# Taking the two-operand elementwise work of one kernel off GpSimd, and opening a stage's PSUM pools in another order

## The chip, the cores and the metric

The kernel runs on one core of a Trainium2 chip. The metric is device time in microseconds, measured from outside the program; the median of three runs is what a version is judged by. One more execution was profiled, and every row below is from that one. [...]

## The reference

One sequence of 512 tokens of width 1024 goes through two blocks in float32. Cut to the order of the work:

```python
# block 1
h = _rms_norm(x, norm_mix_pre);  z = h @ w_in_first
attn = _rms_norm(_dilated_attention(q, k, v), attn_out_gain)
rw = _rwkv7(...)                                  # recurrent scan, 8 heads of 64
mixed = concatenate([attn, rw]) @ w_out
x = x + _rms_norm(mixed, norm_mix_post)
h = _rms_norm(x, norm_ffn_pre)
f = square(relu(h @ w_ffn_up)) @ w_ffn_down       # 1024 -> 4096 -> 1024
x = x + _rms_norm(f, norm_ffn_post)
# block 2
proj = rmsnorm(x) @ w_in                          # conv, q, k, v, gates
x = x + (sigmoid(gate_c) * conv_out + sigmoid(gate_a) * attn_out) @ w_out
x = x + cross_attention(rmsnorm(x), rmsnorm(mem), ...)
x = x + hierarchical_moe(rmsnorm(x), ...)         # 16 experts, two of them per token
return rmsnorm(x, norm_final_g)
```

## The kernel before, in words

**Products.** Activations lie transposed in SBUF (`hT`, 128 features by 512 tokens per tile, two halves of 256 tokens where a norm comes first). A float32 matrix product is made of three products of split operands: hi by hi, lo by hi, hi by lo (lines 371 to 373 with the tokens as the streamed side, lines 380 to 382 with the weights on it). So each weight chunk of 128 x 1024 that a DMA brings (`wl`) is split by `wsplit`: ScalarE (ACT) copies it to a rounded `hi` (L354), and `lo = t - hi` is one elementwise subtraction with two operands in SBUF (L357):

```python
nc.scalar.activation(hi, t, AF.Copy)
self.nsplit += 1
eng = nc.gpsimd if self.nsplit % 4 in SP[self.stage] else nc.vector
eng.tensor_tensor(lo, t, f32(hi), ALU.subtract)
```

The table `SP` (L53) says, by stage, which of four consecutive subtractions go to GpSimd (POOL) and which to VectorE (DVE): two in four while the first mixer's projections, the FFN, the second mixer and the cross-attention's output weights are loaded; all four for the first mixer's `w_out` (whose product runs among the steps of the recurrent scan, `rw_run`) and for the cross-attention's query weights; none for the first low-rank chunk and for the experts. Activations are split in the same manner after a transpose: ACT writes the hi part (L426), DVE the lo part (L427).

**Norms.** A norm that stands behind a product (`post_norm`, L1023 to L1035) handles four row tiles `t` of 128 tokens, twice in block 1 (after `w_out`, on `mix`, and after the FFN, on `f`). For `t` in `PN` (0 and 1), POOL multiplies the tile with the gain (L1029, `mg`), and DVE then does one instruction (L1032). For the other two, DVE does two (L1034: tile times 1/rms times gain; L1035: added to `x`). 1/rms itself is a run of tiny DVE instructions (lines 308 to 326).

**PSUM.** The eight banks are cut anew for each stage by `psum`, which opens pools in the order of its keywords. In the first mixer `mm` has banks 0 and 1, `acc` 2, `s` 3, `tp` 4 and 5, `q` 6 and 7. `ffn` (L1038) opens `mm=5, tp=3`, so its product tiles lie in banks 0 to 4 and its transposes in 5 to 7. The first mixer's `w_out` products leave the `mm` banks through DVE's L688 (`mix`).

**What sets the order.** Functions are generators, interleaved by hand-written tables; a scheduler of the framework then fixes the order of instructions for each engine. At run time every engine takes its own list strictly in that order, and semaphores hold it where an operand or a buffer is not ready. Weight transfers are issued on SP's queue. Lines that the steps below touch: L357 and L354 (splits), L427 and L426, L441 (DVE scales a row for the next norm, `hrow`), L1067 and L1068 (FFN's square of relu and its lo part), L1112 (the convolution's 30 shifted multiply-adds per tile, `cacc`), L519 (a custom DVE instruction, row maximum of attention scores), L512 (PE, scores), L455 and L531 (PE, transposes), L966 (PE, the scan's products), L1241 (gates), L1779 (the last norm's product, on POOL before and after).

Of the kernel before, what the change touches and what calls it, by code (L numbers as in the profile page):

```python
# [36 lines left out]
XW = (7, 2.0)  # L37
XD = 1
CY = (1, 1)
PN = (0, 1)  # L40
RF = ((1, 0, 0), (1, 1, 1), (1, 1, 1))
AH = (3, 14, 3.0, 3, 22, 6.0)
FP, FG = (0,), ((0,), (1, 2), (3,))
# [6 lines left out]
N3 = dict(p=19, w=10, u=10, a=9)  # L50
N4 = dict(p=15, w=16, u=7, wed=3)
PS3 = dict(mm=3, acc=1, s=2, tp=2)
SP = [(), (0, 2), (0, 1, 2, 3), (0, 2), (0, 2), (0, 2), (), (), (0, 2), (0, 2), (0, 1, 2, 3)]  # L53
ENG = {'c16': 's', 'cst': 's', 'mq': 'p', 'mbe': 'p', 'mar0': 'p', 'mar1': 'p', 'mar2': 'p', 'mkv': 'p', 'mx': 'p', 'gs': 's', 'mix': 'p', 'in0': 's', 'in1': 'a', 'in2': 's', 'ma21': 'v', 'gl': 's', 'xl0': 's', 'xl1': 's', 'bk': 'a', 'bv': 'a', 'bb': 'a', 'ba': 'a', 'br': 'a', 'bp': 'a', 'cs': 's', 'cl': 'a', 'xs': 'a', 'hs': 's'}
CAP = 96
NX = 2 * S // CAP
# [5 lines left out]
def f32(ap):  # L62
    return ap.bitcast(F32)


def fl(t):
    return t.rearrange("p a b -> p (a b)")
# [157 lines left out]
class Block:  # L225
# [124 lines left out]
    def wsplit(self, t, tags="hl"):  # L350
# [4 lines left out]
# [3 lines that stand above are left out]
# [665 lines left out]
    def post_norm(self, t, m, gb):  # L1023

        nc = self.nc
        mt, x = fl(m[t]), fl(self.x[t])
        if t in PN:
            mg = fl(self.pt("mg"))
            nc.gpsimd.tensor_tensor(mg, mt, gb, ALU.mult)  # L1029
        r = self.row_rstd(mt, self.junk())  # L1030
        if t in PN:
            nc.vector.scalar_tensor_tensor(x, mg, r[:, 0:1], x, ALU.mult, ALU.add)  # L1032
# [4 lines left out]

    def ffn(self):  # L1038
        with ExitStack() as c:
            self.psum(c, "ff", mm=5, tp=3)  # L1040
            self._ffn()

    def _ffn(self):
# [803 lines left out]
```

## Time and profile before

| | |
|---|---|
| median of three runs | 1493.16 us (1492.92 to 1497.79) |
| the profiled execution: time | 1491.0 us |
| its span (first to last instruction) | 1489.2 us |
| PE busy | 1391.3 us, 93% |
| DVE busy | 865.2 us, 58% |
| ACT busy | 623.2 us, 42% |
| POOL busy | 292.0 us, 20% |
| mean granted PE clock | 0.961 |

The span lies 1.8 us inside the execution's own time, and the execution 2.2 us below the median. A row of the timeline gives start, duration, engine, line, operation and tiles; a bracket at its end is the time for which the engine stood idle before it, and whose result ended that. A merged row (x9) covers the time from the first start to the last end.

### The profile page before, as it was taken

How to read it: one execution, taken by the hardware profiler on the slowest of the kernel's cores; microseconds unless marked ns; L12 is line 12 of the kernel's file. 1: busy time of each engine (PE TensorE's matmuls, PEld its weight loads, DVE VectorE, ACT ScalarE, POOL GpSimd, SP SyncE). 2: the span in 40 equal slices, each digit the busy share in tenths (PEclk: the TensorE clock that was granted, in tenths of full speed). 3: DMA queues.
4: the chain of work that ended last, by engine and by line, in shares of the span. 5: the costliest groups of instructions: out<-in, count | busy, mean ns of one | idle time of the engine just before them, and what ended most of it. 6: DMA issues, size and time to landing. Idle time of an engine off the chain costs nothing. (4 is left out here: it accounts for less than half of the span.)

```text
span 1489.2 us, 21746 instructions
## 1 busy us (share of the span) xinstructions
PE 1391.3 (93%) x8366; PEld 1092.2 (73%) x8366; DVE 865.2 (58%) x1942; ACT 623.2 (42%) x1143; POOL 292.0 (20%) x138
## 2 busy tenths in 40 slices
PE   6999999989789999999998999899999999699996
PEld 5877777766587888888887877667787887466663
DVE  5247655636765144343556575886356356699875
ACT  5344245423244233322444323344432353387873
POOL 2120100011302122212223122111121400222211
PEclk9999999999899999999999999899999998699998
DMA  6231420221213233223233224222122354699994
GB/s 214 85 107 66 126 73 19 75 66 44 71 57 109 65 110 113 74 96 113 89 109 117 68 66 133 72 71 72 57 88 85 97 187 170 220 298 334 335 290 140
DMA packets 67761, 178.02 MB, mean 120 GB/s; under 512 B 17144, under 2 KB 18552, under 8 KB 67648
## 3 DMA queue, kind: packets, MB, share of 16 engines
q1 hardware_dynamic: 58676, 156.39, 31.5%
q0 software_dynamic: 3584, 10.10, 3.1%
q10 hardware_dynamic: 5388, 10.06, 1.9%
q8 instruction: 68, 1.11, 0.3%
q14 instruction: 45, 0.37, 0.1%
HBM read 163.12 MB, written 15.88 MB: 120 GB/s over the span
## 5 line engine op out<-in xcount | busy, mean ns | idle before, releaser
L357 POOL TENSOR_TENSOR ws<-wl,ws 128x1024 fp32r<-128x1024 f32 (+1 forms) x89 | 231.1, 2600 | 925.9 <-ACT ws L354 836.0
L371 PE MATMUL mm<-hT,ws 128*128 128x512 f32 (+3 forms) x872 | 319.0, 370 | 6.3 <-DVE mix L688 4.8
L373 PE MATMUL mm<-hT,ws 128*128 128x512 f32 (+3 forms) x872 | 316.8, 365 | 5.6 <-DVE ws L357 5.6
L354 ACT ACTIVATE ws<-wl 128x1024 fp32r<-128x1024 f32 (+2 forms) x238 | 244.6, 1034 | 178.1 <-PE mm L382 90.2
L372 PE MATMUL mm<-hT,ws 128*128 128x512 f32 (+3 forms) x872 | 317.2, 366 | 1.8 <-DVE hT L427 1.8
L357 DVE TENSOR_TENSOR ws<-wl,ws 128x1024 fp32r<-128x1024 f32 (+2 forms) x149 | 218.1, 1468 | 143.6 <-ACT ws L354 142.0
L371 PEld LDWEIGHTS mm<-hT,ws 128*128 128x128 f32 (+2 forms) x872 | 165.2, 191 | 35.7 <-issue 6.1
L373 PEld LDWEIGHTS mm<-hT,ws 128*128 128x128 f32 (+2 forms) x872 | 165.7, 191 | 32.6 <-DVE ws L357 6.7
L372 PEld LDWEIGHTS mm<-hT,ws 128*128 128x128 f32 (+2 forms) x872 | 165.9, 191 | 28.2 <-DVE hT L427 3.2
L382 PE MATMUL mm<-ws,ff 128*128 128x512 f32 x256 | 100.1, 391 | 0.7 <-DVE ff L1068 0.7
L380 PE MATMUL mm<-ws,ff 128*128 128x512 f32 x256 | 100.0, 391 | 0.0
L381 PE MATMUL mm<-ws,ff 128*128 128x512 f32 x256 | 99.7, 389 | 0.0
L1112 DVE SCALAR_TENSOR_TENSOR cacc<-sig,vec,cacc 128x495 f32<-128x495 f32 (+25 forms) x120 | 92.2, 783 | 1.8
L1067 DVE TENSOR_TENSOR ur<-ur 128x512 f32<-128x512 f32 x32 | 34.7, 1084 | 81.9 <-ACT ff L1066 81.9
L380 PE MATMUL mm<-ws,eh 128*96 128x512 f32 x136 | 56.2, 414 | 1.5 <-ACT eh L423 1.5
L1063 ACT ACTIVATE ur<-mm 128x512 f32<-128x512 f32 x32 | 19.0, 593 | 91.4 <-PE mm L373 91.4
L382 PEld LDWEIGHTS mm<-ws,ff 128*128 128x128 f32 x256 | 48.0, 188 | 12.3 <-DVE ff L1068 2.4
L382 PE MATMUL mm<-ws,eh 128*96 128x512 f32 x136 | 55.7, 409 | 0.7 <-DVE eh L424 0.6
L381 PEld LDWEIGHTS mm<-ws,ff 128*128 128x128 f32 x256 | 48.1, 188 | 10.0
L380 PEld LDWEIGHTS mm<-ws,ff 128*128 128x128 f32 x256 | 48.1, 188 | 9.8
L381 PE MATMUL mm<-ws,eh 128*96 128x512 f32 x136 | 55.0, 405 | 0.0
L521 ACT ACTIVATE sp<-sp,mx 128x128 f32<-128x128 f32 (+3 forms) x64 | 35.6, 558 | 39.7 <-DVE mx L519 39.7
(440 smaller groups left out, 2432.8 us busy)
## 6 DMA issues: line engine op xcount, KB each, us to landing
wl<-w_gu SPq DMA_DIRECT2D x68, 512.0 KB
wl<-w_p SPq DMA_DIRECT2D x60, 512.0 KB
wed<-w_ed SPq DMA_DIRECT2D x68, 256.0 KB
wl<-w_up SPq DMA_DIRECT2D x32, 512.0 KB
wl<-w_dn SPq DMA_DIRECT2D x32, 512.0 KB
wl<-w_out SPq DMA_DIRECT2D x16, 512.0 KB
x<-x SPq DMA_DIRECT2D x8, 512.0 KB
gram_d<-gb SPq DMA_DIRECT2D x8, 256.0 KB
```

Of the source, the lines that this page charges most:

```text
L354: nc.scalar.activation(hi, t, AF.Copy)
L357: eng.tensor_tensor(lo, t, f32(hi), ALU.subtract)
L371: nt.matmul(ps, wh[:, c0:c0 + m], ah[:, sl], start=k == 0, stop=False)
L372: nt.matmul(ps, wh[:, c0:c0 + m], al[:, sl], start=False, stop=False)
L373: nt.matmul(ps, wl[:, c0:c0 + m], ah[:, sl], start=False, stop=k == len(ws) - 1)
L380: nt.matmul(ps, ah[:, sl], wh, start=k == 0, stop=False)
L381: nt.matmul(ps, ah[:, sl], wl, start=False, stop=False)
L382: nt.matmul(ps, al[:, sl], wh, start=False, stop=k == len(ws) - 1)
L521: nc.scalar.activation(sps[h][:, :n], sps[h][:, :n], AF.Exp, scale=-1.0, bias=mxs[h][:, 0:1], accum_out=ls[h])
L1063: nc.scalar.activation(r, ps, AF.Relu)
L1067: nc.vector.tensor_tensor(r, r, r, ALU.mult)
L1112: nc.vector.scalar_tensor_tensor(acc[:, d:], up[:, 0:S - d], w(30 - d), acc[:, d:], ALU.mult, ALU.add)
```

## The change

`PN` becomes empty: all eight norm tiles of block 1 take the two DVE instructions. `SP` becomes empty for every stage: all weight splits are on DVE. `ffn` opens `tp` first: its transposes lie in banks 0 to 2, its product tiles in banks 3 to 7. Eighty-nine splits (87 of 128 x 1024, two of 128 x 16) and four norm products leave POOL; the last norm's product stays there, as do memsets and indirect DMAs.

```diff
-PN = (0, 1)
+PN = ()
...
-SP = [(), (0, 2), (0, 1, 2, 3), (0, 2), (0, 2), (0, 2), (), (), (0, 2), (0, 2), (0, 1, 2, 3)]
+SP = [()] * 11
...
     def ffn(self):
         with ExitStack() as c:
-            self.psum(c, "ff", mm=5, tp=3)
+            self.psum(c, "ff", tp=3, mm=5)
             self._ffn()
```

The order of PE around the FFN's first product, before (`mm_4339` is the last `w_out` product of the first mixer, `mm_4438` the first product tile of the FFN; in brackets the semaphores an instruction waits for):

```order
L382 MATMUL mm_4339<-ws_3965,rT_3846 128x512
L371 MATMUL mm_4438<-hT_4257,ws_4303 128x256 [waits DVE_49,Activation_49]
L372 MATMUL mm_4438<-hT_4257,ws_4303 128x256
L373 MATMUL mm_4438<-hT_4257,ws_4304 128x256
L371 MATMUL mm_4438<-hT_4258,ws_4303 128x256 [waits Activation_49]
```

and now, in the same place:

```order
L382 MATMUL mm_4337<-ws_3965,rT_3846 128x512
L371 MATMUL mm_4436<-hT_4255,ws_4301 128x256 [waits Activation_49]
L372 MATMUL mm_4436<-hT_4255,ws_4301 128x256 [waits DVE_49]
L373 MATMUL mm_4436<-hT_4255,ws_4302 128x256
L371 MATMUL mm_4436<-hT_4256,ws_4301 128x256 [waits Activation_49]
L372 MATMUL mm_4436<-hT_4256,ws_4301 128x256 [waits DVE_49]
```

The order of PE is the same; the first product no longer waits for DVE, and the second term of each chunk now waits for that chunk's lo part.

The order of DVE ahead of the second mixer's first attention unit, before (L519 is the row maximum that the unit's exponentials wait for):

```order
L357 TENSOR_TENSOR ws<-wl,ws 128x2x8 x2
L357 TENSOR_TENSOR ws<-wl,ws 128x1024 x2
L1155 SCALAR_TENSOR_TENSOR fz<-fz,fe 8x512
L1157 SCALAR_TENSOR_TENSOR fe<-one,fz 8x512
L1158 TENSOR_SCALAR fe<-fe 8x512
L357 TENSOR_TENSOR ws<-wl,ws 128x1024 x2
L1110 TENSOR_SCALAR cacc<-sig,vec 128x512
L1112 SCALAR_TENSOR_TENSOR cacc<-sig,vec,cacc 128x511
...
L1112 SCALAR_TENSOR_TENSOR cacc<-sig,vec,cacc 128x503
L1112 SCALAR_TENSOR_TENSOR cacc<-sig,vec,cacc 128x502
L519 ISA sp,mx<-s,cb 128x128
```

and now:

```order
L357 TENSOR_TENSOR ws<-wl,ws 128x2x8 x3
L357 TENSOR_TENSOR ws<-wl,ws 128x1024 x5
L1155 SCALAR_TENSOR_TENSOR fz<-fz,fe 8x512
L1157 SCALAR_TENSOR_TENSOR fe<-one,fz 8x512
L1158 TENSOR_SCALAR fe<-fe 8x512
L357 TENSOR_TENSOR ws<-wl,ws 128x1024 x3
L1110 TENSOR_SCALAR cacc<-sig,vec 128x512
L357 TENSOR_TENSOR ws<-wl,ws 128x1024
L1112 SCALAR_TENSOR_TENSOR cacc<-sig,vec,cacc 128x511
...
L1112 SCALAR_TENSOR_TENSOR cacc<-sig,vec,cacc 128x503
L519 ISA sp,mx<-s,cb 128x128
```

Five more splits of 128 x 1024 stand ahead of that maximum, two of them behind L1158, and nine convolution steps instead of ten. Where the FFN ends and the second mixer begins, DVE's list changes in the same way; before:

```order
L1035 TENSOR_TENSOR x_4203<-x_4203,f_4845 128x1024 [waits DVE_49]
L357 TENSOR_TENSOR ws_7050<-wl_7047,ws_7049 128x1024 [waits DMAHW5_49,Activation_49]
L357 TENSOR_TENSOR ws_7249<-wl_7246,ws_7248 128x1024 [waits DMAHW7_49,PE_49,Activation_49]
L357 TENSOR_TENSOR ws_7261<-wl_7258,ws_7260 128x1024 [waits DMAHW1_49,PE_49,Activation_49]
L427 SCALAR_TENSOR_TENSOR hT_7172<-tp_7180,vec_63,hT_7172 128x256 [waits Activation_49]
```

and now:

```order
L1035 TENSOR_TENSOR x_4201<-x_4201,f_4843 128x1024 [waits DVE_49]
L357 TENSOR_TENSOR ws_7046<-wl_7043,ws_7045 128x1024 [waits DMAHW5_49,Activation_49]
L357 TENSOR_TENSOR ws_7239<-wl_7236,ws_7238 128x1024 [waits DMAHW6_49,PE_49,Activation_49]
L357 TENSOR_TENSOR ws_7245<-wl_7242,ws_7244 128x1024 [waits DMAHW7_49,PE_49,Activation_49]
L357 TENSOR_TENSOR ws_7251<-wl_7248,ws_7250 128x1024 [waits DMAHW0_49,PE_49,Activation_49]
L357 TENSOR_TENSOR ws_7257<-wl_7254,ws_7256 128x1024 [waits DMAHW1_49,PE_49,Activation_49]
L357 TENSOR_TENSOR ws_7503<-wl_7500,ws_7502 128x1024 [waits DMAHW2_49,PE_49,Activation_49]
L427 SCALAR_TENSOR_TENSOR hT_7168<-tp_7176,vec_63,hT_7168 128x256 [waits Activation_49]
```

Six splits instead of three stand ahead of the lo parts (L427) of the next norm's rows, and `ws_7503` belongs to the chunk after the next.

## Rows read from the trace of the kernel before

**Rows 1.** The page, part 1: busy time, share of the span and instructions of each engine.

```profile
PE 1391.3 (93%) x8366; PEld 1092.2 (73%) x8366; DVE 865.2 (58%) x1942; ACT 623.2 (42%) x1143; POOL 292.0 (20%) x138
```

**Rows 2.** Groups by line and shape: busy us, mean ns | idle before, what ended it.

```profile
L357 POOL TENSOR_TENSOR ws<-wl,ws 128x1024 fp32r<-128x1024 f32 x87 | 230.3, 2650 | 908.1 <-ACT ws L354 818.2 <-issue 27.9 <-DVE ws L357 23.0
L357 DVE TENSOR_TENSOR ws<-wl,ws 128x1024 fp32r<-128x1024 f32 x143 | 215.8, 1514 | 137.9 <-ACT ws L354 136.3 <-DMA wed<-w_ed 1.4
...
L1067 DVE TENSOR_TENSOR ur<-ur 128x512 f32<-128x512 f32 x32 | 34.7, 1084 | 81.9 <-ACT ff L1066 81.9
```

**Rows 3.** Timeline, 449 to 459 us, FFN's second chunk: splits on DVE and POOL, and PE.

```profile
449.90 1.23 DVE L357 TENSOR_TENSOR ws<-wl,ws 128x1024 fp32r<-128x1024 f32 x1 [1.26 <-ACT ws L354]
...
454.31 2.47 POOL L357 TENSOR_TENSOR ws<-wl,ws 128x1024 fp32r<-128x1024 f32 x1 [0.31 <-ACT ws L354]
454.47 3.38 DVE L357 TENSOR_TENSOR ws<-wl,ws 128x1024 fp32r<-128x1024 f32 x1
457.91 0.50 PE L373 MATMUL mm<-hT,ws 128*128 128x512 f32 x1 [2.19 <-DVE ws L357]
```

**Rows 4.** Waits of PE: waiting line, for whom: us in total, times, longest.

```profile
PE s L512 <- DVE mx L519: 8.7, 4, 3.9
...
PE mm L371 <- DVE mix L688: 4.8, 1, 4.8
...
PE mm L381 <- POOL ws L357: 3.5, 4, 1.3
```

**Rows 5.** Busy time by stretch, its last columns PEclk, DMA share and GB/s.

```profile
421.00:427.80 6.80, 4.20 (x20) 4.23 (x21) 6.44 (x17) 2.76 (x5) 0.00 (x0) 0.50 0.91 275
393.70:407.40 13.70, 9.36 (x32) 6.65 (x28) 10.88 (x43) 3.57 (x7) 2.35 (x1) 0.50 0.16 41
960.30:967.10 6.80, 5.97 (x16) 4.08 (x17) 5.58 (x14) 1.52 (x4) 0.00 (x0) 0.50 0.01 2
```

**Rows 6.** Timeline, 417 to 438 us, FFN's start: DVE, PE's first product and next transposes.

```profile
417.83 3.22 DVE L357 TENSOR_TENSOR ws<-wl,ws 128x1024 fp32r<-128x1024 f32 x1
...
423.60 0.55 PE L371 MATMUL mm<-hT,ws 128*128 128x256 f32 x1 [4.82 <-DVE mix L688]
...
431.75 1.42 DVE L441 TENSOR_SCALAR hrow<-x,nr_o 128x1024 f32<-128x1024 f32 x2
...
437.05 1.47 PE L455 MATMUL tp<-ident,hrow 128*128 128x128 f32 x12
```

**Rows 7.** Timeline, 390 to 424 us, end of the scan and the norm after `w_out`.

```profile
390.47 2.32 DVE L318 TENSOR_TENSOR nr_q<-nr_o 128x4 f32<-128x4 f32 x1
...
393.38 0.33 PE L966 MATMUL q<-ar,stp 64*64 64x64 f32 x4 [2.44 <-DVE stp L974]
...
423.37 1.22 DVE L1035 TENSOR_TENSOR x<-x,mix 128x1024 f32<-128x1024 f32 x1
```

**Rows 8.** Timeline, 326 to 330, 798 to 803 and 1140 to 1145 us.

```profile
328.40 0.50 PE L381 MATMUL mm<-ws,aA 128*128 128x512 f32 x1 [1.32 <-POOL ws L357]
...
798.76 3.36 DVE L357 TENSOR_TENSOR ws<-wl,ws 128x1024 fp32r<-128x1024 f32 x1
...
802.18 0.39 PE L373 MATMUL mm<-hT,ws 128*128 128x256 f32 x1 [3.38 <-DVE ws L357]
...
1144.59 0.50 PE L380 MATMUL mm<-ws,mg 128*128 128x512 f32 x1 [1.37 <-ACT mg L426]
```

**Rows 9.** Timeline, 920 to 992 us, the second mixer's attention: DVE's convolution and PE's scores.

```profile
928.59 0.33 PE L531 MATMUL tp<-ident,sp 128*128 128x128 f32 x1 [2.52 <-DVE sp L525]
...
949.50 2.86 DVE L1112 SCALAR_TENSOR_TENSOR cacc<-sig,vec,cacc 128x484 f32<-128x484 f32 x1
...
961.13 0.79 PE L512 MATMUL s<-kT,qT 64*128 64x128 f32 x2 [3.86 <-DVE mx L519]
...
991.30 2.55 PE L512 MATMUL s<-kT,qT 64*128 64x512 f32 x4 [3.44 <-DVE mx L519]
```

**Rows 10.** Waits of POOL: waiting line, for whom: us in total, times, longest.

```profile
POOL ws L357 <- ACT ws L354: 836.0, 72, 114.8
```

## The prediction, made before the changed kernel ran

> **What bounds the kernel now.** I read the page's first part, the groups, PE's waits, the busy time by stretch, and then the timeline around the longest stops of PE. PE is busy in 93% of the span and no other engine in over 58% [rows 1], so the kernel is bound by PE, and the change does not touch what PE does. It can only shorten PE's stops, or lengthen them. [...]
>
> Why PE stops is seen in one place [rows 3]. A split of 128 x 1024 takes DVE 1.23 us when it is alone. At 454.47 the same instruction took 3.38 us: it began 0.16 us behind a POOL split of 2.47 us and ended 1.07 us behind it, about what it needs by itself. PE stood 2.19 us for it. The groups say that this is common: the 143 DVE splits have a mean of 1514 ns, the 87 POOL splits one of 2650 [rows 2]. So POOL's help is slow, and it holds DVE while it runs. I read this as: a DVE instruction that reads two SBUF operands waits for the end of a POOL instruction of that kind.
>
> **What the change adds to DVE.** 87 x 1.23 = 107 us of splits (the two of 128 x 16 are too small to count), and four norm products, whose price is one more instruction of 1.22 us each, as L1035 shows [rows 7], 5 us. What DVE gets back is at least 143 x (1.514 - 1.23) = 41 us in its own splits; L1067 with its mean of 1084 ns and convolution steps such as the one of 2.86 us [rows 2, 9] gain as well. So DVE's busy time grows by at most 112 - 41 = 71 us, to 936 of some 1480, 63%. The average leaves room; the question is what stands ahead of an urgent instruction in DVE's list.
>
> [...] Were each POOL instruction to cost DVE its whole length, 91 of them by 2.65 us would give DVE 241 us back and its busy time would fall; the mean of 1514 ns says that most of them meet no such instruction.
>
> **The sum, place by place.**
>
> *FFN's start.* PE's first product waited 4.82 us for L688, which emptied a bank that the FFN's product tiles took over [rows 4, 6]. With the pools in the other order that product has no such wait. The lo parts it needs next (L427) stand behind a DVE split that took 3.22 us at 417.83 beside POOL and would take 1.23, so they come 2 us sooner. What is late next: the transposes for tokens 257 to 512 (L455), which need the rows that L441 ended at 431.75 + 1.42 = 433.17; PE reached them at 437.05, so 3.9 us can be won before that wait opens, and a little more since DVE is earlier too. Between nothing and 4.8, I take 4.
>
> *FFN's later chunks.* The stop of 2.19 us [rows 3] goes with its POOL split. Between nothing and 2.2, I take 2. The rest of the FFN costs nothing: DVE's extra splits lie beside PE, which runs there without stops; should that cover go, each would be 1.23.
>
> *The scan and the norm behind it.* All of `w_out` is split on POOL there. PE waited four times for POOL's splits, 3.5 us in all [rows 4], once 1.32 at 328.40 [rows 8]. A tiny DVE instruction, L318, took 2.32 us beside POOL's norm product and let PE stand 2.44 [rows 7]. Both go. Against them, 16 splits enter DVE's list among the scan's steps, 16 x 1.23 = 20 us, and the norm's two more instructions 2.4 us. Each can hold up a step by at most its 1.23 us. If one in three does, that costs 16/3 x 1.23 = 6.6, and what was won is about gone. Between +5.9 (all gained) and -6, I take +3, nearer to the gain, as PE's wait for POOL comes to an end by construction and DVE was held by POOL anyway.
>
> *The border of FFN and second mixer.* The split at 798.76 took 3.36 us and PE stood 3.38 [rows 8]. Now six splits instead of three stand ahead of the next norm's lo parts, one of them for a later chunk. Between -1.2 (one split that need not be there) and +3.4, I take +1.
>
> *The second mixer's attention.* PE stood 2.52, 3.86 and 3.44 us [rows 9], 9.8 in all, each time for a row maximum (L519) or what follows it, with convolution steps and splits ahead of it on DVE, some of them stretched by POOL (2.86 at 949.50). One convolution step fewer, none stretched, but more splits: between nothing and 9.8, I take 5.
>
> *Output product.* The 1.37 us at 1144.59 [rows 8], which came of one gate instruction beside a POOL split: between 0 and 1.4, I take 1.
>
> *The clock.* Of the 9.8 us behind three stops I take 6: the stretch at the FFN's start should go, the other two in part.
>
> Sum: 4 + 2 + 3 + 1 + 5 + 1 + 6 = 22. The profiled execution took 1491.0 us, so 1469.0 there; it lies 2.2 us below the median of the runs, so the forecast is 1471. The upper ends are 4.8 + 2.2 + 5.9 + 3.4 + 9.8 + 1.4 + 9.8 = 37, the lower ones -7.
>
> **Rivals.**
>
> *A. DVE takes over the stops.* POOL's slowness goes, but in the scan and the attention DVE's own list is now as long, and the same stops stay. What is left is the FFN's start, its second chunk and half of one stretch of slow clock: 4 + 2 + 2 = 8, 1485. For it: the attention's maximum has five more splits ahead of it in the first place. Against it: four splits at 1.23 are less than two stretched to 3.4.
>
> *B. All of it, and more.* Every stop named goes and the clock stays up: 37 us, 1456, and some more where other stops of the kind, not in my rows, go too. For it: the one instruction at 454.47, if it is typical. Against it: the mean of 1514 ns.
>
> *C. Slower, by what stands in line on DVE.* POOL waited 836 us in 72 waits for ACT's hi parts, once for 114.8 [rows 10]. That harmed no one, as nothing urgent stood behind it. On DVE a split whose hi part or buffer isn't there holds everything behind it: the lo parts of a norm, the row maxima, the scan's steps. The likely places are the chunk borders of the second mixer, where a split of the chunk after next now stands ahead of the lo parts. One such stop costs as the attention's do, 3.86 and 3.44, some 3.6 us, and the clock as much again (half of a stretch of 6.8 us, 3.4), so 7. From four new ones (28) the gain of 22 is gone and it gets slower; at five it is 1493 + 35 - 22 = 1506. For it: rows 10. Against it: the waits of L357 on DVE are already 137.9 us idle for ACT [rows 2], beside a PE that stops for splits only in single places, and the scheduler put the splits where it expected their operands.
>
> [...]
>
> *D. No change.* The bank wait turns into a wait for the lo parts, and POOL's stops into DVE's, one for one: 1493.
>
> **How the numbers follow.** The forecast case, 1457 to 1481: 0.61. Rival A, 1481 to 1488.7: 0.19. Rival B, below 1457: 0.08. Rival D: 0.07. Rival C: 0.05. A measurement tells about 0.3% (4.5 us) from no change, so below 1488.7 is faster and above 1497.6 slower: faster 0.61 + 0.19 + 0.08 = 0.88, within 0.07, slower 0.05. The range reaches from 1457, leaving out B's 0.08, to 1488, leaving out C, D and the edge of A.
>
> **What the next profile would show.** If right: no POOL row of L357 nor L1029; the DVE splits at a mean near 1.23 us with 230 of 128 x 1024; DVE busy 890 to 936 us; no wait of L371 for L688, FFN's first product at most 1 us behind the last `w_out` product; no stop at the FFN's second chunk; attention stops of about half, 9.8 to 5. PE's busy time falls by the slow stretches that are gone. A would show the attention's and the scan's stops at their old lengths with DVE named. C would show new waits of PE for L427 or L519, and DVE idle ahead of a split for ACT. The prediction is wrong if DVE's splits stay long without POOL beside them, for then my reading of rows 3 falls, or if the first product of the FFN still stands 4 us for something else.

## The result, and the profile after

The changed kernel takes 1447.7 us (median of four runs, 1445.0 to 1450.0) against 1493.0 of the kernel before (1480.9 to 1497.8): 0.970 of its time, 95% interval 0.965 to 0.974. That is faster by 45 us, where 22 were forecast, and below the range. In three later comparisons the changed kernel took 0.972, 0.974 and 0.975 of before, 37 to 43 us less, so 45 is at the upper end.

The first part of the page of the changed kernel, to be read against [rows 1]:

```profile
span 1443.2 us, 21699 instructions
...
PE 1370.2 (95%) x8366; PEld 1080.2 (75%) x8366; DVE 875.6 (61%) x2035; ACT 623.8 (43%) x1143; POOL 51.3 (4%) x45
```

PE runs the same 8366 matmuls, in another order only in short runs within the scan and the second mixer, with 21 us less of busy time, and POOL has nearly nothing left. DVE has 93 instructions more, and is busy for only 10.4 us more, although 87 splits at 1.22 and four norm instructions at 1.22 came to it, 111 us. So some 100 us came back to it. The groups by line and shape of the changed kernel, against [rows 2], show where from:

```profile
L357 DVE TENSOR_TENSOR ws<-wl,ws 128x1024 fp32r<-128x1024 f32 x230 | 278.1, 1222 | 135.0 <-ACT ws L354 128.5 <-PE mm L373 1.2 <-DMA wl<-w_gu 0.4
...
L1067 DVE TENSOR_TENSOR ur<-ur 128x512 f32<-128x512 f32 x32 | 22.1, 692 | 82.3 <-ACT ff L1066 82.3
```

The mean of a split fell from 1514 to 1222 ns, that of L1067 from 1084 to 692: 42 and 13 us. The rest is spread over the convolution (the longest step of L1112 took 2.87 us before and takes 0.75 now) and many small groups.

PE's waits in the changed kernel, against [rows 4]: waiting line, for whom, us in total, times, longest.

```profile
PE tp L455 <- DVE hrow L441: 16.7, 5, 10.7
...
PE mm L381 <- DVE ws L357: 1.7, 2, 1.4
...
PE s L512 <- DVE mx L519: 1.3, 4, 0.6
...
PE mm L372 <- DVE hT L427: 1.0, 1, 1.0
```

The wait for L688 is gone, L512's went from 8.7 us to 1.3, the wait of L381 for POOL's splits became one for DVE's of 1.7. The places one by one. First the FFN's start, timeline of the changed kernel from 413 to 429 us, against [rows 6]:

```profile
414.22 1.21 DVE L357 TENSOR_TENSOR ws<-wl,ws 128x1024 fp32r<-128x1024 f32 x1
...
414.80 0.39 PE L382 MATMUL mm<-ws,rT 128*128 128x512 f32 x1
...
415.03 0.28 PE L371 MATMUL mm<-hT,ws 128*128 128x256 f32 x1
...
427.90 0.33 PE L455 MATMUL tp<-ident,hrow 128*128 128x128 f32 x1 [1.20 <-DVE hrow L441]
```

The FFN's first product follows the last `w_out` product without a stop, the split ahead of the lo parts takes 1.21 us instead of 3.22, and what is late next is L455 for L441, by 1.20 us. In the second mixer's attention the same stretch of PE's program took 83.5 us before and 64.7 now. Busy time by stretch (the columns of [rows 5]; PEclk is the granted share of the full clock of TensorE, PE in the rows, and the clock's records in these two profiles read 0.50 or 1.00), before:

```profile
917.70:1001.20 83.50, 73.67 (x338) 52.73 (x338) 76.09 (x143) 29.31 (x65) 12.32 (x6) 0.88 0.23 77
```

and after:

```profile
897.70:962.40 64.70, 64.01 (x340) 46.60 (x340) 62.78 (x132) 28.29 (x61) 0.00 (x0) 1.00 0.27 88
```

Before, DVE was busy for 91% of this stretch, and now for 97%, with PE at 99%: here, unlike in the mean over the kernel, the two engines are tied. DVE has eleven instructions fewer in it and none stretched, 13.3 us less; PE's stops went from 9.8 us to 0.7, and the clock from 0.88 to 1.00. That the two are tied is read from these rows; no run changed DVE's sum here alone. One of the three stops, at its place in the changed kernel's timeline, against [rows 9]:

```profile
929.28 1.22 DVE L357 TENSOR_TENSOR ws<-wl,ws 128x1024 fp32r<-128x1024 f32 x1
930.41 0.69 DVE L519 CUSTOM_DVE_ANT_0 sp<-s,cb 128x512 f32<-128x512 f32 x1
...
931.16 0.48 PE L512 MATMUL s<-kT,qT 64*128 64x128 f32 x2 [0.19 <-DVE mx L519]
```

The maximum still stands behind a split, and PE waits 0.19 us for it instead of 3.86.

The table adds up where the 45 us came from. Both profiles are cut at the starts of the same PE instructions; "stops" are the times with no matmul running. The rest of a difference, 21 us in all, is PE running slower or faster; the granted clock accounts for some 20 of it.

| stretch of before, us | time before | time after | difference | of it stops | rest |
|---|---|---|---|---|---|
| 0 to 285, first mixer | 285.1 | 288.0 | +2.9 | +1.0 | +1.8 |
| 285 to 413, end of scan, norm | 127.9 | 121.5 | -6.5 | -3.9 | -2.6 |
| 413 to 500, FFN's start | 87.0 | 77.3 | -9.7 | -5.6 | -4.0 |
| 500 to 780, rest of FFN | 280.1 | 278.7 | -1.4 | -0.5 | -0.9 |
| 780 to 890, border, second mixer | 109.9 | 104.6 | -5.3 | -3.6 | -1.7 |
| 890 to 1005, attention | 115.0 | 96.9 | -18.1 | -9.1 | -9.0 |
| 1005 to 1090 | 85.0 | 86.9 | +1.9 | -0.2 | +2.1 |
| 1090 to 1300, output, cross-attention, routing | 210.1 | 201.6 | -8.5 | -2.1 | -6.5 |
| 1300 to the last product, experts | 175.1 | 174.4 | -0.7 | -0.4 | -0.3 |

The scan's row holds for this profile alone: in the other three of the changed kernel it came to -0.1, +1.7 and 0.0 us, as the clock took back what the stops gave there (-5.9 to -6.2), while the rows from 413 to 1005 repeat within 0.6 us. All stops together fell from 73.3 to 48.8 us, by 24.5. The mean granted clock rose from 0.961 to 0.974, so what was lost by the clock fell from 0.039 x 1489 = 58 us to 0.026 x 1443 = 38, by some 20. The two make up the difference.

### The profile page after: what moved, and what is told of

Same layout as the page of the kernel before. It is cut to its first block, busy times and chain, and to the rows that moved or that the text cites. A ratio compares the mean times of both kernels' runs of the same rounds, so it can differ in the third digit from the quotient of the medians.

```text
span 1443.2 us, 21699 instructions
## 1 busy us (share of the span) xinstructions
PE 1370.2 (95%) x8366; PEld 1080.2 (75%) x8366; DVE 875.6 (61%) x2035; ACT 623.8 (43%) x1143; POOL 51.3 (4%) x45
## 4 chain that ended last, share of the span: by engine, by line
PE 82%; DVE 10%; DMA 3%; ACT 2%; issue 2%; SPq 0%; DVEq 0%; ACTq 0%
PE mm L371 11%; PE mm L372 11%; PE mm L373 11%; PE mm L380 10%; PE mm L382 10%; PE mm L381 10%; PE q L966 3%; DVE ws L357 2%; PE mm L1720 2%; PE acc L537 1%; PE s L512 1%; PE tp L531 1%; DVE cacc L1112 1%; PE tp L917 1%; PE mm L917 1%
## 5 line engine op out<-in xcount | busy, mean ns | idle before, releaser
L357 DVE TENSOR_TENSOR ws<-wl,ws 128x1024 fp32r<-128x1024 f32 (+2 forms) x238 | 280.7, 1192 | 141.2 <-ACT ws L354 134.6
L371 PE MATMUL mm<-hT,ws 128*128 128x512 f32 (+3 forms) x872 | 314.7, 365 | 1.7 <-ACT qT L565 0.7
L372 PE MATMUL mm<-hT,ws 128*128 128x512 f32 (+3 forms) x872 | 314.4, 363 | 1.1 <-DVE hT L427 1.0
L373 PE MATMUL mm<-hT,ws 128*128 128x512 f32 (+3 forms) x872 | 313.0, 361 | 0.0
L371 PEld LDWEIGHTS mm<-hT,ws 128*128 128x128 f32 (+2 forms) x872 | 162.4, 188 | 30.1 <-ACT qT L565 1.4
L372 PEld LDWEIGHTS mm<-hT,ws 128*128 128x128 f32 (+2 forms) x872 | 163.2, 188 | 27.2 <-DVE hT L427 2.1
L373 PEld LDWEIGHTS mm<-hT,ws 128*128 128x128 f32 (+2 forms) x872 | 163.0, 187 | 24.9 <-DVE ws L357 0.2
L381 PE MATMUL mm<-ws,ff 128*128 128x512 f32 x256 | 99.6, 389 | 0.0
L1112 DVE SCALAR_TENSOR_TENSOR cacc<-sig,vec,cacc 128x507 f32<-128x507 f32 (+25 forms) x120 | 86.1, 733 | 1.6
L1067 DVE TENSOR_TENSOR ur<-ur 128x512 f32<-128x512 f32 x32 | 22.1, 692 | 82.3 <-ACT ff L1066 82.3
L381 PEld LDWEIGHTS mm<-ws,ff 128*128 128x128 f32 x256 | 48.1, 188 | 9.9
L381 PE MATMUL mm<-ws,eh 128*96 128x512 f32 x136 | 54.7, 402 | 0.0
L1086 DVE TENSOR_TENSOR f<-f,mm 128x512 f32<-128x512 f32 x24 | 16.4, 685 | 49.2 <-PE mm L382 49.2
```

The costliest lines, as they stand in the source:

```text
L371: nt.matmul(ps, wh[:, c0:c0 + m], ah[:, sl], start=k == 0, stop=False)
L372: nt.matmul(ps, wh[:, c0:c0 + m], al[:, sl], start=False, stop=False)
L373: nt.matmul(ps, wl[:, c0:c0 + m], ah[:, sl], start=False, stop=k == len(ws) - 1)
L381: nt.matmul(ps, ah[:, sl], wl, start=False, stop=False)
L1112: nc.vector.scalar_tensor_tensor(acc[:, d:], up[:, 0:S - d], w(30 - d), acc[:, d:], ALU.mult, ALU.add)
```

## The experiments

The theory to test: a two-operand elementwise instruction on POOL holds DVE's instructions on SBUF, and these held PE. The rivals: POOL's splits came late by themselves, DVE's new order is the better one, or the bank order did most of it.

**The change in three parts.** The kernel before with one part of the change each.

```diff
# x1_banks
-            self.psum(c, "ff", mm=5, tp=3)
+            self.psum(c, "ff", tp=3, mm=5)
# x2_norm
-PN = (0, 1)
+PN = ()
# x3_splits
-SP = [(), (0, 2), (0, 1, 2, 3), (0, 2), (0, 2), (0, 2), (), (), (0, 2), (0, 2), (0, 1, 2, 3)]
+SP = [()] * 11
```

> Only the order of the FFN's PSUM pools is changed; POOL keeps its splits and norm products. Theory 1 (the gain comes of DVE no longer being held by POOL): the 4.82 us stop for L688 goes, but the lo parts still stand behind a DVE split of 3.2 us, so a new stop of 1 to 3 us for L427 or L357 takes its place; 2 to 6 us faster than before, about 1488, and the attention's stops of 2.5, 3.9 and 3.4 us stay. Rival (the banks are a large part of it, through the clock behind the stop): 8 to 10 us, about 1484.

> Only the norm products go to DVE; splits and banks as before. Theory 1: the 2.44 us stop of L966 beside POOL's norm product goes and perhaps the slow stretch behind it, 2 to 6 us faster, about 1489. Rival (POOL's products cost nothing, as the splits do it all): within 2 us of before.

> Only the splits go to DVE; norm products and banks as before. Theory 1: 32 to 40 us faster, about 1456, no stop over 1 us in the attention (before 2.5, 3.9 and 3.4), DVE splits at a mean near 1.2 us. Rival (banks and norm products carry half of it): 20 us faster, about 1473.

The banks: 1478.7 us, 0.990 of before (0.986 to 0.993). The norm products: 0.999 (0.996 to 1.003), no difference. The splits: 1456.2 us, 0.976 (0.972 to 0.981), 37 us. So it is the splits above all, as theory 1 has it, and the attention's stops of 2.5, 3.9 and 3.4 us went with them alone: its stretch fell by the same 18.2 us. The norm products took away the stop of 2.44 us beside POOL's product, and others of 1 to 2.2 us around the norm took its place. The banks gave more than theory 1 had, and in this comparison more than the rival's 8 to 10. The timeline of the kernel with the new banks alone, 417 to 422 us:

```profile
417.81 3.26 DVE L357 TENSOR_TENSOR ws<-wl,ws 128x1024 fp32r<-128x1024 f32 x1
...
418.60 0.28 PE L371 MATMUL mm<-hT,ws 128*128 128x256 f32 x1
...
421.51 0.39 PE L372 MATMUL mm<-hT,ws 128*128 128x256 f32 x1 [0.84 <-DVE hT L427]
```

PE starts at once, works on those chunks whose lo parts are there, and stops only 0.84 us behind the long split: 3.8 us are won in the stretch from 413 to 500 us. The other 8 or so lie elsewhere, mostly by the clock: 1.5 at the border, 1.0 in the attention and 5.6 between 1090 and 1300 us. That is taken up below.

**Work for nobody on POOL.** The changed kernel; where POOL had done a split, it now reads one column of the hi part, as pace, and subtracts a scratch tile from itself. Nobody reads the result. The order of instructions on PE, DVE, ACT and SP is the changed kernel's.

```diff
+        nc.gpsimd.tensor_copy(gh[:, 0:1], f32(hi)[:, 0, 0:1])
+        nc.gpsimd.tensor_tensor(gh, gh, gh, ALU.subtract)
```

> The changed kernel, and beside each of the 89 splits that POOL did before POOL now does two instructions on a scratch tile that nobody reads: one of 128 x 1, which reads one column of the hi part and so paces it, and one subtraction of 128 x 960 whose operands and result lie in the scratch tile. Theory 1 (a POOL instruction that reads SBUF holds DVE): DVE's splits go back to a mean of 1.4 to 1.5 us, PE's stops at the second mixer's attention and at the border come back, and 20 to 40 us of the gain are lost, 1468 to 1488. Theory 2 (POOL's splits were late, or stood in a better place on DVE's list now; holding DVE matters little): within 5 us of the changed kernel, 1443 to 1453, since nobody waits for the scratch tile and the order on every other engine is that of the changed kernel.

1496.7 us (1493.5 to 1503.2), 1.002 of before (1.000 to 1.004): the whole gain is gone, and more than theory 1 had expected. The groups of this kernel:

```profile
L357 DVE TENSOR_TENSOR ws<-wl,ws 128x1024 fp32r<-128x1024 f32 x230 | 343.9, 1513 | 124.8 <-ACT ws L354 123.0 <-DMA wed<-w_ed 0.2
L358 POOL TENSOR_TENSOR gh<-gh 128x960 bf16<-128x960 bf16 x89 | 195.2, 2194 | 7.1
```

The splits are back at a mean of 1513 ns, and DVE at 978.5 us busy, 103 more than in the changed kernel, for the same instructions. The timeline of the FFN's second chunk in this kernel:

```profile
460.72 2.12 POOL L358 TENSOR_TENSOR gh<-gh 128x960 bf16<-128x960 bf16 x1
461.12 2.80 DVE L357 TENSOR_TENSOR ws<-wl,ws 128x1024 fp32r<-128x1024 f32 x1
...
463.98 0.50 PE L373 MATMUL mm<-hT,ws 128*128 128x512 f32 x1 [2.95 <-DVE ws L357]
```

It is the picture of [rows 3] again: DVE's split ends 1.08 us behind POOL's, and PE stands for it. The attention's stops are back at the same three places, of 3.1, 2.8 and 2.2 us, with one of 4.2 at the border. In PE's waits of this kernel:

```profile
PE s L512 <- DVE mx L519: 5.7, 4, 2.8
PE tp L531 <- DVE sp L525: 5.3, 3, 3.1
```

PE and DVE wait for nothing of POOL's in this kernel, and ACT only for the pace instruction, 3.1 us in nine places. So that POOL's splits were late is ruled out as the main cause, and so is the new order on DVE and PE, which this kernel has as well.

**The same with writes alone.** Three memsets of the scratch tile in place of the subtraction.

```diff
-        nc.gpsimd.tensor_tensor(gh, gh, gh, ALU.subtract)
+        for _ in range(3): nc.gpsimd.memset(gh, 0.0)
```

> As the run with the reading scratch work, but POOL's subtraction is replaced by three memsets of the same scratch tile, which write SBUF and read nothing; the instruction of 128 x 1 that reads the hi part stays as pace. Theory 1a (it is the reading of SBUF by POOL that holds DVE): within 5 us of the changed kernel, 1443 to 1455, DVE splits at a mean near 1.22 us. Theory 1b (any POOL instruction holds it): 1475 to 1500, splits at 1.4 to 1.5 us.

1455.1 us (1449.0 to 1456.9), 0.972 of before (0.967 to 0.976), which overlaps the changed kernel's 0.965 to 0.974. The groups:

```profile
L357 DVE TENSOR_TENSOR ws<-wl,ws 128x1024 fp32r<-128x1024 f32 x230 | 278.2, 1222 | 135.2 <-ACT ws L354 132.4
L358 POOL MEMSET gh<- 128x960 bf16 x267 | 241.2, 903 | 15.6
```

POOL is busier than in the run above, 350 us against 318, and the splits stay at 1222 ns. So it is not POOL at work as such that holds the splits: beside the scratch work that reads SBUF they took 1513 ns, beside the one whose long instructions only write 1222. That is as theory 1a has it, whose upper bound of 1455 the time just meets. ACT's wait for the pace instruction is there too, 3.7 us, so that is not what made the run above slow.

**Which stage.** The changed kernel with the old table for some stages.

```diff
-SP = [()] * 11
# x6_mixer2_back
+SP = [(), (), (), (), (0, 2), (), (), (), (), (0, 2), ()]
# x7_ffn_back
+SP = [(), (), (), (0, 2), (), (), (), (), (0, 2), (), ()]
# x8_scan_back
+SP = [(), (), (0, 1, 2, 3), (), (), (), (), (), (), (), ()]
```

> The changed kernel with the second mixer's splits back on POOL by the old table (stages 4 and 9). Theory 1: PE's stops of 2.5, 3.9 and 3.4 us in the attention and of 3.4 at the border come back with two or three slow stretches; 16 to 24 us slower than the changed kernel, about 1467. Rival (the gain is spread evenly over the program): 30 of 89 splits, a third of 45, so 15 us, and no stop over 2 us in the attention.

> The changed kernel with the FFN's splits back on POOL (stages 3 and 8), banks as changed. Theory 1: one stop of 2.2 us in the second chunk comes back with its slow stretch, and the lo parts at the FFN's start are 2 us late; 4 to 8 us slower, about 1454, although 32 splits are moved. Rival (evenly spread): 32 of 89 splits, 16 us, 1464.

> The changed kernel with the splits of the first mixer's output weights back on POOL (stage 2). Two sides: PE's four waits for POOL there, 3.5 us, come back, but DVE's list among the scan's steps is 20 us shorter, and the slow stretches that the changed kernel shows at 365 to 376 us (5 us lost) may go. Theory 1 with the scan bound by DVE's list: 0 to 6 us faster than the changed kernel, about 1445. Rival (POOL holds the scan's small DVE instructions): 3 to 8 us slower, about 1453.

Second mixer: 1467.3 us, 0.981 (0.973 to 0.988); 26 large splits went back. The page's waits show L512 at its old length, and the stretch of the attention that takes 64.7 us in the changed kernel takes 83.4 here, 18.7 more, 9.1 of it stops:

```profile
PE s L512 <- DVE mx L519: 8.2, 4, 3.9
```

The stop at the border did not come back, against theory 1; that the total came out as it said is in part luck, as the clock in the scan cost this profile 10 us more than the first one of the changed kernel. FFN: 1460.4 us, 0.976 (0.971 to 0.981); 35 large splits went back, which cost 5.8 us at the FFN's start, 1.4 in the rest of the FFN and 2.1 at the border. The second chunk of this kernel:

```profile
452.68 2.46 POOL L357 TENSOR_TENSOR ws<-wl,ws 128x1024 fp32r<-128x1024 f32 x1 [0.32 <-ACT ws L354]
452.84 3.39 DVE L357 TENSOR_TENSOR ws<-wl,ws 128x1024 fp32r<-128x1024 f32 x1
...
456.28 0.50 PE L373 MATMUL mm<-hT,ws 128*128 128x512 f32 x1 [2.21 <-DVE ws L357]
```

The whole loss, 12.7 us, is above the 4 to 8 that the theory had; the profile puts another 5.8 us into the scan, where this kernel does the same as the changed one, and there it is the clock. Three of the four profiles of the changed kernel have that loss in the scan as well, 6.4 to 8.2 us above the first; against the changed kernel's mean over all comparisons, 1450.8 us, the FFN's splits cost 9.6. Scan: 1445.0 us, 0.968 (0.963 to 0.973), not slower. So the price of a split on POOL depends on its stage: dear in the attention and at the FFN's start, small in the rest of the FFN, and none among the scan's steps. The rival that the gain is spread evenly falls for the attention.

**Is the scan better off with POOL?** The changed kernel, the one with the scan's splits back, one with the first mixer's as well, and one with the old banks.

```diff
# x11_mixer1_scan_back, against the changed kernel
-SP = [()] * 11
+SP = [(), (0, 2), (0, 1, 2, 3), (), (), (), (), (), (), (), ()]
# x12_old_banks, against the changed kernel
-            self.psum(c, "ff", tp=3, mm=5)
+            self.psum(c, "ff", mm=5, tp=3)
```

> The changed kernel itself, on the same chip as the three below, for comparison. 0.970 of before by every theory; from run to run the time should follow the granted clock, some 3 to 5 us for each 0.003 of it.

> The changed kernel with the splits of the first mixer's output weights (stage 2) on POOL, once more. If the first look was the mechanism: 2 to 6 us faster than the changed kernel beside it, with no slow stretch of over 2 us between 340 and 390 us. If it was chance of the clock: within 2 us of it.

> As the run above, and the first mixer's projections (stage 1) on POOL by the old table too. The changed kernel lost about 1.9 us against before in its first 60 us, where splits on DVE stand in the second half of the norm. If that comes of these splits: 1 to 2 us faster than the run above. If POOL holds DVE's small instructions there as elsewhere: 0 to 3 us slower.

> The changed kernel with the old order of the FFN's pools (mm first). With splits and norm products on DVE the wait for L688 was 1.8 us in the run with splits alone. Theory: the bank wait is mostly a DVE wait and is short when nothing holds DVE: 2 to 4 us slower than the changed kernel. Rival (banks by themselves are worth the 14 us that they brought on top of before): 8 to 14 us slower.

Medians: 1450.2 for the changed kernel, 1446.6 with the scan's splits on POOL, 1446.5 with the first mixer's as well, 1455.1 with the old banks. The first mixer's splits make no difference that can be told. The old banks cost 4.9 us beside the changed kernel, a little above the 2 to 4 expected, but the intervals overlap (0.971 to 0.979 against 0.969 to 0.976 of before); the wait is there, shorter than in [rows 4]:

```profile
PE mm L371 <- DVE mix L688: 2.8, 1, 2.8
```

A third comparison of the scan, and one with half of its splits:

```diff
# x15_scan_half, against the changed kernel
-SP = [()] * 11
+SP = [(), (), (0, 2), (), (), (), (), (), (), (), ()]
```

> The changed kernel with two of four of the scan's splits (stage 2) on POOL. If the stretch at 340 to 390 us follows the DVE splits among the scan's steps: less than 5 us lost there, and 1 to 4 us faster than the changed kernel beside it. If not: within 2 us of it, with 5 to 17 us lost there.

> The changed kernel beside the others. By every theory 0.970 of before; a slow stretch between 340 and 390 us again, of 5 to 17 us.

> The changed kernel with the scan's splits (stage 2) on POOL, beside the changed kernel itself. If the scan's slow stretch is worth having back: its median lies 2 to 5 us below the one beside it and the stretch at 340 to 390 us costs under 4 us. If it was chance: within 1.5 us.

> The changed kernel, for the run above. A slow stretch of 5 to 19 us lost between 340 and 390 us; 1446 to 1455 us.

Half: 1451.4 against 1454.3 of the changed kernel beside it, 3 us faster with 10 us still lost in the stretch, so in part like either expectation. All: 1447.5 against 1453.6. Over all comparisons the changed kernel has 22 executions with a mean of 1450.8 us, and the one with the scan's splits on POOL 15 with 1447.0: 3.7 us less, give or take 2.7. This version beats both kernels, by little over the changed one. The reason is in the clock. Busy time by stretch, 340 to 390 us, in the second profile of the changed kernel:

```profile
340.00:390.00 50.00, 46.43 (x463) 34.02 (x459) 30.29 (x101) 14.20 (x36) 0.00 (x0) 0.66 0.18 57
```

and in the first of the kernel with the scan's splits on POOL:

```profile
340.00:390.00 50.00, 43.62 (x542) 32.12 (x540) 32.51 (x130) 18.07 (x45) 9.92 (x5) 1.00 0.21 65
```

In each of the four profiles of the changed kernel PE ran at half clock (0.50) for a part of this stretch, losing 5, 17, 19 and 17 us; with half of the splits on POOL 10; with all of them there (three profiles, and one more with the first mixer's) at most 3.4, and in both profiles of the kernel before none. Over all profiles, the ten with all of these splits on DVE lost 5 to 19 us there, and the nine with all of them on POOL at most 3.4. That the splits on DVE go with it is shown; why it turns up there and not before the change, where PE's stops are as many, isn't.

**Does the clock follow the kernel?** The kernel before and the banks alone, profiled once more.

> The kernel before, profiled once more. If the slow stretch at 1247 to 1261 us follows the kernel: it is there again, 5 to 8 us lost. If it differs from execution to execution: its length differs by more than 3 us, or it is absent, with PE's stops there unchanged.

> The bank order alone, once more. The place itself gave 3.9 us in its first profile. If the distant stretches follow the kernel: again 12 to 15 us faster than before, and no stretch at 803 us nor of over 2 us near 1245 us. If not: 4 to 9 us faster, 1485 to 1489.

The kernel before again: the same stretch near half clock (0.54), from 1246 to 1261 us, 6.8 us lost in either profile:

```profile
1246.00:1261.00 15.00, 14.47 (x58) 12.44 (x58) 7.70 (x33) 4.73 (x15) 0.00 (x0) 0.54 0.39 147
```

The banks alone again, the same place of the program, which it reaches half a us earlier:

```profile
1245.50:1260.50 15.00, 13.63 (x82) 11.36 (x83) 10.79 (x43) 6.95 (x20) 0.00 (x0) 1.00 0.56 195
```

So in these two profiles of each kernel the stretch follows the kernel, and yet the two stops of PE ahead of it (0.89 and 0.52 us in all four profiles) are the same. The time did not repeat as well: the banks alone took 1484.9 us this time, 0.994 (0.991 to 0.997), a hair beyond the 4 to 9 us of the second expectation, while the stretches at 803 and 1245 us are absent, as in the first; over both comparisons their gain is 9 to 15 us. The kernel before beside itself came to 0.997 (0.994 to 1.000), which tells how far such a ratio can be off.

## Why the prediction was wrong

Right was that a POOL split holds DVE and DVE holds PE. The scratch work shows it: with the subtraction on POOL the splits on DVE took 1513 ns and the kernel 1496.7 us, without it 1222 ns and 1447.7 us. Right too were the sign and, of the places, the FFN's: 6 us of stops taken for its start and second chunk, 5.6 measured, with L441 late next, as foretold. DVE's busy time came out at 875.6 us, below the 890 to 936 forecast: POOL had held more than the splits (L1067 went from 1084 to 692 ns). Wrong were sizes. Of the 23 us that the forecast missed, some 14 are the clock's term, and 8.5 are stops (24.5 measured, 16 taken), half of them in the attention.

- **"Between nothing and 9.8, I take 5", for the attention.** 9.1 us of stops went. The step that failed is the weighing of DVE's list there by what stands ahead of a maximum (one convolution step fewer, none stretched, but more splits). In that stretch DVE was busy for 91% of the time, and the sum of all that it does there fell by 13.3 us; that this sum sets the pace, and not what stands just ahead of one maximum, is how I read it. A window of 83 us over the busy time by stretch would have shown the 91%; the prediction had put DVE at 63% in the mean and stopped there.
- **"Of the 9.8 us behind three stops I take 6", for the clock.** Some 20 us came back. No run shows the 9.8 us as such: they are the author's estimate, half of the time for which PE was busy in the three stretches at 0.50 of [rows 5]; what the profiles showed in their place is a loss by the clock of 58 us before and 38 after. The step that failed is the count of slow stretches. The term has three; but PE was at half clock (0.50) behind four other stops that the prediction names as well, in the second chunk, at the border, and at the first and third stop of the attention:

```profile
458.60:462.00 3.40, 3.40 (x10) 2.62 (x9) 1.78 (x3) 1.23 (x2) 0.00 (x0) 0.50 0.78 260
803.30:806.70 3.40, 3.40 (x18) 3.40 (x18) 0.00 (x0) 0.09 (x1) 0.00 (x0) 0.50 0.82 290
929.60:936.40 6.80, 6.80 (x17) 4.79 (x18) 6.24 (x16) 1.36 (x5) 0.00 (x0) 0.50 0.01 5
991.00:997.80 6.80, 6.50 (x18) 4.32 (x19) 5.90 (x16) 2.22 (x7) 0.00 (x0) 0.50 0.38 139
```

That is another 10 us. These four went in the changed kernel, and two of the three that were counted: 9.0 us in the attention, 4.0 at the FFN's start with its second chunk, 1.7 at the border. The third, in the scan, stayed, 6.8 us long instead of 13.7. Another 6.5, between 1090 and 1300 us, follow no stop that the change removed in that place. In all, the profile of before has 58 us lost by the clock (0.039 of 1489).
- **The border, +1.** 3.6 us of stops went: the six splits ran with nothing to hold them, and the lo parts behind them were only 0.97 us late.
- **The scan and the norm, +3.** 3.9 us of stops measured, near. But that is in part luck: 16 splits were counted on DVE's list, and eight is what the stage has; and in three of four profiles of the changed kernel the clock takes back all of it.
- **The smaller ones:** the output product and what follows it gave 2.1 us of stops where 1 was taken; the rest of the FFN came to 1.4 where nothing was; and the first 285 us lost 1.0 in stops and 1.8 by the clock, which no term had.

Of the rivals, B was nearest: every stop named goes and the clock stays up, 1456 "and some more where other stops of the kind, not in my rows, go too". It was given 0.08, against it "the mean of 1514 ns". That mean says how often a split is held, not whether the few held ones are those that PE waits for. A did not come about. C, in which a split waits on DVE for its hi part, did not either: DVE's idle time ahead of L357 for ACT was 136.3 us for 143 splits and is 128.5 for 230. Waits of that kind were there before the change too (DVE stood idle for 9.48 us ahead of the split at 911.35 us), but after it nothing urgent was behind a waiting split for long: PE's longest wait for L427 was 1.0 us, for L519 0.6.

## What to carry to other kernels

Work given to GpSimd to relieve VectorE may hardly relieve it: here 89 splits and four norm products on GpSimd spared VectorE 10 us of 876, as the splits left on VectorE took 1514 ns in the mean beside it instead of 1222. A subtraction on GpSimd, which reads SBUF, was enough to bring them back to 1513 ns; memsets alone left them at 1222. Compare the mean time of the same VectorE instruction with its shortest, and where they differ, price the offload by the instructions that it holds and by who waits for those. Judge whether VectorE has room in each stretch by itself; 58% over the kernel was 91% where it mattered. And count a stop of TensorE with the slow stretch behind it: here the clock gave back some 20 us and the stops 24.5.

## What the runs showed of the hardware

- A subtraction of 128 x 960 on POOL, which reads SBUF, beside the splits made their mean on DVE 1513 ns; with three memsets of the same tile in its place, which only write, it was 1222, as in the changed kernel, where POOL has neither.
- In the run with memsets two DVE instructions with one operand were longer: L1137 took up to 1.08 us (at most 0.43 in the changed kernel) and L926, a copy, up to 1.04 (0.22), while the longest of the 230 large splits took 1.23 us in either. From that run's timeline:

```profile
858.17 2.01 POOL L358 MEMSET gh<- 128x960 bf16 x2
858.26 1.08 DVE L1137 TENSOR_SCALAR sig<-sig 128x512 f32<-128x512 f32 x1
```

- POOL's instructions were longer beside DVE's too. POOL's pace instruction of 128 x 1 took 0.19 us at its shortest and 3.31 us when DVE did three splits in a row beside it, from 956.24 to 959.73 us; its mean was 773 ns in the first of the two runs with scratch work. From that run's timeline, where the second row has the last two of the three splits:

```profile
956.46 3.31 POOL L358 CAST gh<-ws 128x1 bf16<-128x1 f32 x1 [25.62 <-ACT ws L354]
957.37 2.35 DVE L357 TENSOR_TENSOR ws<-wl,ws 128x1024 fp32r<-128x1024 f32 x2
```

- The clock doesn't follow the stops alone. With the same two stops of 0.89 and 0.52 us at the same place of the program, PE ran at 0.54 of its clock for 15 us in both profiles of the kernel before, and in the two with only the banks changed it kept its full clock (1.00) there in one and had 0.89 over 15 us in the other. One of these reaches the place six us earlier than before, the other less than one; the cause stays open. And one program differs from profile to profile at another place: 5 to 19 us lost in the scan in four profiles of the changed kernel.
